# Heads' square sums as four-strip groups between the halves of a projection, and heads' row scales as one float32r product over stacked halves

## The chip, the cores and the metric

The kernel runs on one core of one Trainium2 chip. The metric is device time of one execution in microseconds (us), lower is better. A core has TensorE (PE: matrix products, which land in PSUM), VectorE (DVE), ScalarE (ACT), GpSimd (POOL) and the sync engine (SP), which here only issues transfers. Each engine works through its own list of instructions in order; engines wait for one another by semaphores. An instruction that waits holds up everything behind it on its engine.

## The reference, cut to what matters

One decoder layer for 512 prompt rows and 64 sample rows (576 together) that share weights. The part that the change touches is the QK norm of the attention branch: every head of q (16) and k (4) is scaled, row by row, by one over the root of the mean of its 64 squares.

```python
def rmsnorm(x, w):
    xf = x.astype(jnp.float32)
    y = xf * lax.rsqrt(jnp.mean(xf * xf, axis=-1, keepdims=True) + RMS_EPS)
    return (y * w.astype(jnp.float32)).astype(x.dtype)
...
z, xbc, dt_raw, q, k, v, f_raw, g_ssd, g_att = split_combined(xn @ p['w_in'])
...
q = rmsnorm(q.reshape(b, L, ATT_HEADS, ATT_HEAD_DIM), p['q_norm'])
k = rmsnorm(k.reshape(b, L, KV_HEADS, ATT_HEAD_DIM), p['k_norm'])
```

## The kernel before, in words

Activations lie transposed: 128 channels on the partitions, the 576 rows along the free axis, cut into two halves of 288. A projection multiplies a 128-column weight tile (split by `split` into float32r halves `whi` and `wlo`) with the activations (`xh`, `xl`): `mm3` (lines 207 to 215) issues three products for each of eight tiles of the contraction, 24 for each half of the rows, at lines 212, 213 and 214. These "main" products are most of PE's work all through the program. `project` (line 664) calls `mm3` for the two halves, each into its own PSUM tile `acc`, and DVE moves each half out, times the row scale `rbc` (line 669).

Ten projections make 128-channel tiles of two heads each: two of k, then eight of q (here: pair 0 to pair 9), then two tiles of v. After each of the ten, `squares` has ACT square the tile: the prompt columns into a tile of 512 columns (`Ls`, line 682), the sample columns into 64 columns of `kk` (line 683). After pairs 3, 7 and 9 it writes the products that sum the squares of each head (line 689): for each pair one full-float32 product of a 128x32 selector (`hE`, in `cst`) with the 512 columns, and one with the 64, each into its own strip of 32 PSUM partitions: pair j goes to strip j mod 4. Below, "strip product" is such a product with 512 columns.

From the sums DVE makes one over the root (`rsqrt`, line 766 on: `hs_`, transposes, `xr_`, result `yr` or `PT`). PE transposes that back to 24 partitions x 576 (lines 771 and 774), DVE copies it into `hr` (float32). `headnorm` (line 700) spreads two heads' rows of `hr` over 128 partitions by a float32 product with a 24x128 selector (line 703, 512 columns), and DVE multiplies the tile by it (line 704). It is called for the two k tiles and for q tile 0 before the attention loop, and for q tiles 1 to 7 inside it, one in every fourth step. The 64 sample columns of the two k tiles (line 787) and of all eight q tiles (line 817) are done before the loop, four times two products for q.

While this chain runs, PE is kept busy by further projections (`beside`): pieces of the gate and z projections are issued as filler. The Tile scheduler decides the order on each engine from a cost model, with `soon()` raising priority and `behind(a, b)` forbidding a ahead of b; inside the attention loop PE's order is the written one (`manual_schedule`).

Of the kernel before, what the change touches and what calls it, by code (L numbers as in the profile page):

```python
# [14 lines left out]
F32 = mybir.dt.float32  # L15
F32R = mybir.dt.float32r
I32 = mybir.dt.int32
AF = mybir.ActivationFunctionType
ALU = mybir.AluOpType
# [4 lines left out]
P = 128  # L24
OFFSET = 3000
D = 1024
NP = 512
NS = 64
NT = NP + NS
# [64 lines left out]
def build(ctx, tc, A, O):  # L94
    nc = tc.nc
    uid = [0]

    def tl(pool, shape, dt=F32, tag=None, bufs=None):
        uid[0] += 1
        kw = {} if bufs is None else {"bufs": bufs}  # L100
        return pool.tile(shape, dt, tag=tag, name=f"{tag}_{uid[0]}", **kw)
# [4 lines left out]
    mm = nc.tensor.matmul  # L106
    act = nc.scalar.activation
    V = nc.vector
    G = nc.gpsimd
# [12 lines left out]
    ident = tl(constp, [P, P], tag="ident")  # L122
    nc.scalar.dma_start(out=ident, in_=A["consts"][:, :P])

    def C(n, rows=P):
        o, w = COFF[n]
        return cst[:rows, o - P:o - P + w]
# [4 lines left out]
    def tr():  # L132
        return bank("tr", 2)

    def sm():
        return bank("mm", 2)

    def pv():
        return bank("pv", 2)
# [13 lines left out]
    def behind(later, first):  # L153

        tc.add_manual_dep(later.ins, first.ins.name, mybir.DependencyInfo(mybir.DependencyClass.NoSync, mybir.DependencyReason.DATA), reason="order")
# [51 lines left out]
    def mm3(out, w, xs, half, first=True, last=True):  # L207

        n = len(w)
        for i, ((hi, lo), (xh, xl)) in enumerate(zip(w, xs)):  # L210
            a, b = xh[:, hs(half)], xl[:, hs(half)]
            mm(out, lhsT=hi, rhs=a, start=first and i == 0, stop=False)  # L212
            mm(out, lhsT=hi, rhs=b, start=False, stop=False)  # L213
            end = mm(out, lhsT=lo, rhs=a, start=False, stop=last and i == n - 1)  # L214
        return end
# [202 lines left out]
    with pool("h1", reuse_waits="tile") as hp:  # L418
        hts = [tl(hp, [P, NT], tag=f"h{k}") for k in range(8)]
        nrm1 = Norm(0)  # L420
        with pool("xin", side="right", reuse_waits="tile") as xi:
# [4 lines left out]
            for half in range(2):  # L426
                d = slice(half * (D // 2), (half + 1) * (D // 2))
                for c in range(5):
                    n = P if c < 4 else NS
# [5 lines left out]
            t = tr()  # L435
            nc.tensor.transpose(t[:, :8], r1, ident[:8, :8])
            V.tensor_copy(P1[:, :8], t[:, :8])
            for k in range(8):
                t = tr()
# [6 lines left out]
                t = sm()  # L446
# [5 lines left out]
            for c in range(5):  # L452
                n = P if c < 4 else NS
# [6 lines left out]
        with pool("setup2", side="right", reuse_waits="tile") as su:  # L460
            q = nc.scalar
# [14 lines left out]
            t = tr()  # L476
# [7 lines left out]
            t = tr()  # L484
# [7 lines left out]
            t = tr()  # L492
# [87 lines left out]
    xs, rbc = nrm2.xs, nrm2.r  # L580
# [21 lines left out]
    with pool("dtf", side="right", reuse_waits="tile") as dp:  # L602
        w = []
        for k in range(0, 8, 4):
# [3 lines left out]
            hi, lo = split(stg, 4, 48)  # L608
            w += [(hi[:, i, :], lo[:, i, :]) for i in range(4)]
        x0 = tl(dp, [48, NT], tag="x0")  # L610
        for half in range(2):
            a = pv()
# [5 lines left out]
        e = tl(dp, [48, NT], tag="e")  # L618
# [23 lines left out]
        for c in range(5):  # L642
            n = P if c < 4 else NS
            t = tr()
# [17 lines left out]
    with pool("att", side="right", reuse_waits="tile") as ap:  # L662

        def project(w, out):
            for half in range(2):
                a = acc()
                mm3(a, w, xs, half)
                with soon():
                    V.tensor_tensor(out[:, hs(half)], a, rbc[:, hs(half)], ALU.mult)

        hp_, hq_ = pv(), sm()
        nhead = [0]

        sqs = tl(ap, [P, 10, NS], tag="kk", bufs=3)
        sqp = []

        def squares(kf):

            j = nhead[0]
            nhead[0] += 1  # L680
            sqp.append(tl(ap, [P, NP], tag="Ls", bufs=7))
            act(sqp[j], kf[:, :NP], AF.Square)
            act(sqs[:, j, :], kf[:, NP:], AF.Square)
            if j % 4 < 3 and j < 9:
                return
            for out, sq in ((hp_, lambda i: sqp[i]), (hq_[:, :NS], lambda i: sqs[:, i, :])):
                for i in range(j // 4 * 4, j + 1):
                    c, m = i % 4, i // 4
                    mm(out[c * 32:(c + 1) * 32], lhsT=C("hE")[:, 18 - 2 * m:50 - 2 * m], rhs=sq(i), start=m == 0, stop=i > 5)

        def row_of(j):
            return j % 4 * 6 + j // 4 * 2

        def heads(j, tag="bias", bufs=4):

            sel = tl(ap, [24, 2, 64], tag=tag, bufs=bufs)
            G.tensor_copy(sel, ident[:24, row_of(j):row_of(j) + 2].unsqueeze(2).to_broadcast([24, 2, 64]))
            return sel.rearrange("k e m -> k (e m)")

        def headnorm(kf, sel, wcol):  # L700
# [5 lines left out]
        def tokens(src, dst_p, dst_s, keep):  # L706
# [12 lines left out]
                res.append(o)  # L719
            return res  # L720

        kc, vc = Cols(win, CK), Cols(win, CV)
        kfs = []
        for p in range(2):
# [5 lines left out]
        for p in range(2):  # L730
            for g2 in range(0, 4, 2):
# [9 lines left out]
                for gi in range(2):  # L741
                    w = []
# [18 lines left out]
        t, t2 = tr(), sm()  # L761
# [3 lines left out]
        V.tensor_copy(xr_[:, :4], t.rearrange("p (c q r) -> p c q r", c=4, q=4)[:, :, :, :6])  # L765
        V.tensor_copy(xr_[:, 4], t2[:, :P].rearrange("p (q r) -> p q r", q=4)[:, :, :6])
        yr = rsqrt(xr_.rearrange("p c q r -> p (c q r)"), 120, ap, (("L", 4), ("PT", 2), ("Ls", 7)))
        hr = tl(ap, [24, NT], tag="hr")
        t = tr()
        for c in range(4):  # L770
            nc.tensor.transpose(t[:24, c * P:(c + 1) * P], yr[:, c * 24:(c + 1) * 24], ident)
        V.tensor_copy(hr[:, :NP], t[:24])
        t = tr()
        nc.tensor.transpose(t[:24, :P], yr[:, 96:120], ident)
        V.tensor_copy(hr[:, NP:], t[:24, P - NS:P])
        sel8 = tl(ap, [24, 8, 2, 64], tag="vv", bufs=3)
        for j, n in ((2, 2), (4, 4), (8, 2)):
            o = row_of(j)
            G.tensor_copy(sel8[:, j - 2:j - 2 + n], ident[:24, o:o + 6 * n].rearrange("k (q r) -> k q r", r=6)[:, :, :2]
                          .unsqueeze(3).to_broadcast([24, n, 2, 64]))  # L780
        khat, khs, sels = kfs, [], []
        for p in range(2):
            sels.append(heads(p))
# [772 lines left out]
```

## Time and profile before

| what | value |
|---|---|
| median of 3 runs | 1865.89 us (1864.46 to 1866.64) |
| the profiled execution | 1864.62 us, of which the trace's span is 1862.8 us |
| granted TensorE clock, mean | 0.996 of full |
| DVE, ACT, POOL busy | 56%, 41%, 34% of the span |

Times in the trace count from the span's start. A row of the timeline gives start, length, engine, line, operation, output <- inputs, shapes and how many records it merges ("x2"); in square brackets the idle time of the engine just before it and what ended that. Matrix products overlap in PE's pipeline, so what one costs is the distance between starts, not its length: six main products from 494.53 to 495.33 are 0.133 us each, though each row says 0.29. A full-float32 product leaves two records, a float32r product one.

The part of the program spoken of: pairs 0 to 9 are projected up to 541 us, v up to 548, filler from there to 605 (with `hr` ready at 573.6), then the attention loop up to about 870.

### The profile page before, as it was taken

How to read it: one execution, taken by the hardware profiler on the slowest of the kernel's cores; microseconds unless marked ns; L12 is line 12 of the kernel's file. 1: busy time of each engine (PE TensorE's matmuls, PEld its weight loads, DVE VectorE, ACT ScalarE, POOL GpSimd, SP SyncE). 2: the span in 40 equal slices, each digit the busy share in tenths (PEclk: the TensorE clock that was granted, in tenths of full speed). 3: DMA queues.
4: the chain of work that ended last, by engine and by line, in shares of the span. 5: the costliest groups of instructions: out<-in, count | busy, mean ns of one | idle time of the engine just before them, and what ended most of it. 6: DMA issues, size and time to landing. Idle time of an engine off the chain costs nothing.

```text
span 1862.8 us, 38777 instructions
## 1 busy us (share of the span) xinstructions
PE 1827.1 (98%) x15335; PEld 1724.5 (93%) x15335; DVE 1050.9 (56%) x2281; ACT 754.9 (41%) x1571; POOL 626.4 (34%) x697
## 2 busy tenths in 40 slices
PE   8999999999999999999999999989999999999998
PEld 7999999999889888888998898878999999999998
DVE  4643334443425777776737968787676454344542
ACT  4333223333323555555426555555433333123322
POOL 0433002212322445543324544746454222002210
PEclk9999999999999999999999999999999999999999
DMA  4644443344525688775356545354473344554342
GB/s 149 163 124 136 132 140 103 114 139 138 145 72 172 194 240 246 225 226 173 91 158 184 140 126 144 108 148 135 132 226 93 118 120 128 148 146 119 108 123 65
DMA packets 297723, 269.72 MB, mean 145 GB/s; under 512 B 55068, under 2 KB 262092, under 8 KB 297388
## 3 DMA queue, kind: packets, MB, share of 16 engines
q1 hardware_dynamic: 229712, 184.16, 35.0%
q10 hardware_dynamic: 57828, 46.10, 8.0%
q0 software_dynamic: 10000, 36.97, 6.2%
q8 instruction: 121, 1.98, 0.4%
q14 instruction: 62, 0.51, 0.1%
HBM read 223.72 MB, written 38.73 MB: 141 GB/s over the span
## 4 chain that ended last, share of the span: by engine, by line
PE 87%; DVE 6%; DMA 3%; ACT 2%; issue 1%; ACTq 1%; POOL 0%; SPq 0%; DVEq 0%; POOLq 0%
PE acc L212 16%; PE acc L213 16%; PE acc L214 16%; PE pv L213 8%; PE pv L212 8%; PE pv L214 8%; PE tr L962 2%; PE tr L949 1%; PE mm L885 1%; DMA ab<-cumD 1%; DVE kf L1187 1%; PE pv L916 1%; PE pv L1358 1%; PE mm L903 1%; PE pv L1000 1%
## 5 line engine op out<-in xcount | busy, mean ns | idle before, releaser
L176 ACT ACTIVATE whi<-stage 128x512 fp32r<-128x512 f32 (+2 forms) x474 | 294.3, 622 | 696.0 <-PE acc L213 606.3
L212 PE MATMUL acc<-xh,whi 128*128 128x288 f32 x1792 | 540.9, 302 | 9.0 <-DVE xr L1161 5.6
L213 PE MATMUL acc<-xl,whi 128*128 128x288 f32 x1792 | 531.2, 296 | 0.0
L214 PE MATMUL acc<-xh,wlo 128*128 128x288 f32 x1792 | 531.2, 297 | 0.0
L177 DVE TENSOR_TENSOR wlo<-stage,whi 128x512 fp32r<-128x512 f32 (+1 forms) x373 | 271.5, 728 | 251.4 <-ACT whi L176 242.6
L212 PEld LDWEIGHTS acc<-xh,whi 128*128 128x128 f32 x1792 | 337.7, 188 | 16.5 <-DVE xr L1161 7.9
L213 PEld LDWEIGHTS acc<-xl,whi 128*128 128x128 f32 x1792 | 337.9, 189 | 1.7 <-issue 1.4
L214 PEld LDWEIGHTS acc<-xh,wlo 128*128 128x128 f32 x1792 | 337.2, 188 | 2.1 <-issue 1.5
L348 POOL TENSOR_TENSOR u<-u,s 128x288 f32<-128x288 f32 x88 | 82.1, 934 | 436.6 <-DVE u L347 378.0
L177 POOL TENSOR_TENSOR wlo<-stage,whi 128x512 fp32r<-128x512 f32 (+1 forms) x101 | 138.8, 1375 | 265.7 <-ACT whi L176 248.8
L212 PE MATMUL pv<-xh,whi 128*128 128x288 f32 (+1 forms) x720 | 213.8, 297 | 0.0
L213 PE MATMUL pv<-xl,whi 128*128 128x288 f32 (+1 forms) x720 | 212.4, 295 | 0.0
L214 PE MATMUL pv<-xh,wlo 128*128 128x288 f32 (+1 forms) x720 | 212.0, 295 | 0.0
L213 PEld LDWEIGHTS pv<-xl,whi 128*128 128x128 f32 (+1 forms) x720 | 134.5, 187 | 1.3
L212 PEld LDWEIGHTS pv<-xh,whi 128*128 128x128 f32 (+1 forms) x720 | 134.6, 187 | 0.4
L214 PEld LDWEIGHTS pv<-xh,wlo 128*128 128x128 f32 (+1 forms) x720 | 134.5, 187 | 0.2
L212 PE MATMUL pv<-hh,whi 128*128 128x288 f32 x352 | 105.7, 300 | 0.0
L213 PE MATMUL acc<-hl,whi 128*128 128x288 f32 x352 | 104.1, 296 | 0.0
L212 PE MATMUL acc<-hh,whi 128*128 128x288 f32 x352 | 104.1, 296 | 0.0
L213 PE MATMUL pv<-hl,whi 128*128 128x288 f32 x352 | 104.1, 296 | 0.0
L214 PE MATMUL acc<-hh,wlo 128*128 128x288 f32 x352 | 104.1, 296 | 0.0
L214 PE MATMUL pv<-hh,wlo 128*128 128x288 f32 x352 | 103.8, 295 | 0.0
(366 smaller groups left out, 3601.7 us busy)
## 6 DMA issues: line engine op xcount, KB each, us to landing
stage<-in_w_in_dram SPq DMA_DIRECT2D x52, 512.0 KB
stage<-in_ffn_w_up_dram SPq DMA_DIRECT2D x44, 512.0 KB
stage<-in_ffn_w_gate_dram SPq DMA_DIRECT2D x43, 512.0 KB
stage<-in_ffn_w_down_dram SPq DMA_DIRECT2D x40, 512.0 KB
h<-in_state_ssm_dram SPq DMA_DIRECT2D x64, 256.0 KB
hTD<-hT ACTq DMA_DIRECT2D x32, 256.0 KB
pb<-pastD SPq DMA_DIRECT2D x32, 256.0 KB
ab<-cumD SPq DMA_DIRECT2D x32, 256.0 KB
```

What stands on the lines that cost most here:

```text
L176: act(hi, view, AF.Copy)
L177: e.tensor_tensor(lo, view, hi.bitcast(F32), ALU.subtract)
L212: mm(out, lhsT=hi, rhs=a, start=first and i == 0, stop=False)
L213: mm(out, lhsT=hi, rhs=b, start=False, stop=False)
L214: end = mm(out, lhsT=lo, rhs=a, start=False, stop=last and i == n - 1)
L348: G.tensor_tensor(u, u, sil[half], ALU.mult)
L885: mm(s[:, :n], lhsT=q, rhs=ks[2 * self.p + e][:, :n], start=hl == 0, stop=hl == 1)
L903: nc.tensor.transpose(t[:, j * P:(j + 1) * P], lt[:, j * P:(j + 1) * P], ident)
L916: mm(self.ob[o:o + 32, i * P:(i + 1) * P], lhsT=vtok[j][:, v0:v0 + 32], rhs=self.pts[e][:, j * P:(j + 1) * P], start=j == 0, stop=j == i)
L949: nc.tensor.transpose(t[:, i * P:(i + 1) * P], kk[:, i, p * P:(p + 1) * P], ident)
L962: mm(s[kv * 32:(kv + 1) * 32, :], lhsT=self.q(kv), rhs=self.kT[kv // 2], start=True, stop=True)
L1000: mm(ob[kv * 32:(kv + 1) * 32, :64], lhsT=self.pt[:, i * P + kv * 32:i * P + (kv + 1) * 32], rhs=vv[:, i, kv * 64:(kv + 1) * 64], start=jq ...
```

## The change

It has two parts. First, `squares` no longer writes the strip products at once; it puts a function `emit` on a list, and the next `project` calls it between its two halves. `emit` chains its products, each `behind` the one before it, the first behind the last product of half 0, and half 1 begins behind the last of them. Second, `hr` holds float32r values on 128 partitions: rows 0 to 23 the scales rounded to float32r, rows 32 to 55 what the rounding left, the rest zero. The selectors take both (`id2` is the sum of two shifted pieces of the identity), so one float32r product over 128 partitions replaces the float32 product over 24. The stacked halves come from two DVE copies of `yr` into `y2`, five transposes with 64 output rows, an ACT copy and a DVE subtraction.

```diff
 def mm3(...):
-            mm(out, lhsT=hi, rhs=a, start=first and i == 0, stop=False)
+            begin = mm(out, lhsT=hi, rhs=a, start=first and i == 0, stop=False)
+            if i == 0:
+                mm3.begin = begin
...
         def project(w, out):
             for half in range(2):
                 a = acc()
-                mm3(a, w, xs, half)
+                end, begin = mm3(a, w, xs, half), mm3.begin
+                if half == 0 and strips:
+                    end = strips.pop()(end)
+                elif half == 1:
+                    behind(begin, before)
+                before = end
...
         def squares(kf):
...
-            for out, sq in ((hp_, lambda i: sqp[i]), (hq_[:, :NS], lambda i: sqs[:, i, :])):
-                for i in range(j // 4 * 4, j + 1):
-                    c, m = i % 4, i // 4
-                    mm(out[c * 32:(c + 1) * 32], lhsT=C("hE")[:, 18 - 2 * m:50 - 2 * m], rhs=sq(i), start=m == 0, stop=i > 5)
+            def emit(x):
+                for out, sq in ((hp_, lambda i: sqp[i]), (hq_[:, :NS], lambda i: sqs[:, i, :])):
+                    for i in range(j // 4 * 4, j + 1):
+                        c, m = i % 4, i // 4
+                        y = mm(out[c * 32:(c + 1) * 32], lhsT=C("hE")[:, 18 - 2 * m:50 - 2 * m], rhs=sq(i), start=m == 0, stop=i > 5)
+                        behind(y, x)
+                        x = y
+                return x
+            strips.append(emit)
...
         def heads(j, tag="bias", bufs=4):
-            sel = tl(ap, [24, 2, 64], tag=tag, bufs=bufs)
-            G.tensor_copy(sel, ident[:24, row_of(j):row_of(j) + 2].unsqueeze(2).to_broadcast([24, 2, 64]))
+            sel = tl(ap, [P, 2, 64], F32R, tag=tag, bufs=bufs)
+            G.tensor_copy(sel, id2[:, row_of(j):row_of(j) + 2].unsqueeze(2).to_broadcast([P, 2, 64]))
...
+        hr = tl(ap, [P, NT], F32R, tag="hr")
+        G.memset(hr.bitcast(F32)[64:], 0.0)
+        y2 = tl(ap, [P, 5, 64], tag="Ls", bufs=7)
+        G.memset(y2, 0.0)
+        id2 = tl(ap, [P, 32], tag="id2")
+        G.tensor_tensor(id2, ident[:, :32], ident[:, 32:64], ALU.add)
+        sel8 = tl(ap, [P, 8, 2, 64], F32R, tag="vv", bufs=3)
...
-        hr = tl(ap, [24, NT], tag="hr")
-        t = tr()
-        for c in range(4):
-            nc.tensor.transpose(t[:24, c * P:(c + 1) * P], yr[:, c * 24:(c + 1) * 24], ident)
-        V.tensor_copy(hr[:, :NP], t[:24])
-        t = tr()
-        nc.tensor.transpose(t[:24, :P], yr[:, 96:120], ident)
-        V.tensor_copy(hr[:, NP:], t[:24, P - NS:P])
-        sel8 = tl(ap, [24, 8, 2, 64], tag="vv", bufs=3)
...
+        for e in range(2):
+            V.tensor_copy(y2[:, :, 32 * e:32 * e + 24], yr.rearrange("p (c r) -> p c r", c=5))
+        t, t2 = tr(), tr()
+        for c in range(5):
+            nc.tensor.transpose(t[:64, c * P:(c + 1) * P] if c < 4 else t2[:64, :P], y2[:, c, :], ident)
+        for o, v in ((hr[:, :NP], t), (hr[:, NP:], t2[:, P - NS:P])):
+            act(o[:64], v[:64], AF.Copy)
+            V.tensor_tensor(o[32:64], v[32:64], o[32:64].bitcast(F32), ALU.subtract)
```

PE's list of before, at the first group: half 1 of pair 4 (`acc_5862`) has begun when the strip products of pairs 0 to 3 come (`Ls_5604`, `Ls_5668`, `Ls_5742`, `Ls_5806`); `kk_5538` is the tile with the sample columns.

```order
L214 MATMUL acc_5862<-xh_4810,wlo_5828 128x288
L689 MATMUL pv_5536<-Ls_5604,cst_75 32x512
L689 MATMUL mm_5537<-kk_5538,cst_75 32x64
L212 MATMUL acc_5862<-xh_4910,whi_5827 128x288
L689 MATMUL pv_5536<-Ls_5668,cst_75 32x512
L213 MATMUL acc_5862<-xl_4911,whi_5827 128x288
L689 MATMUL mm_5537<-kk_5538,cst_75 32x64
L214 MATMUL acc_5862<-xh_4910,wlo_5828 128x288
L212 MATMUL acc_5862<-xh_5002,whi_5827 128x288
L213 MATMUL acc_5862<-xl_5003,whi_5827 128x288
L689 MATMUL pv_5536<-Ls_5742,cst_75 32x512
```

PE's list of the changed kernel at the same place: the last product of half 0 of pair 4 (`acc_5838`), the group, then half 1 (`acc_5872`).

```order
L216 MATMUL acc_5838<-xh_5359,wlo_5834 128x288
L700 MATMUL pv_5536<-Ls_5614,cst_75 32x512
L700 MATMUL pv_5536<-Ls_5678,cst_75 32x512
L700 MATMUL pv_5536<-Ls_5752,cst_75 32x512
L700 MATMUL pv_5536<-Ls_5816,cst_75 32x512
L700 MATMUL mm_5537<-kk_5538,cst_75 32x64 x4
L212 MATMUL acc_5872<-xh_4717,whi_5829 128x288
```

The four strip products stand together, six main products earlier than the first of them stood, and no main product is between them. Pairs 4 to 7 and pairs 8 and 9 are grouped likewise, where before each of these six stood alone among main products.

ACT's list of before at the same place: the squares of pairs 0 to 3 follow a weight split (`whi`) and a row of transfer issues (DMA).

```order
L649 DMA out_dram<-TT_911_5401 128x16
L176 ACTIVATE whi_5895<-stage_5822 128x512
L682 ACTIVATE Ls_5604<-qy_5539 128x512
L683 ACTIVATE kk_5538<-qy_5539 128x64
L682 ACTIVATE Ls_5668<-qy_5607 128x512
L683 ACTIVATE kk_5538<-qy_5607 128x64
L682 ACTIVATE Ls_5742<-qy_5689 128x512
```

ACT's list of the changed kernel there.

```order
L651 DMA out_dram<-TT_911_5401 128x16
L176 ACTIVATE whi_5905<-stage_5824 128x512
L691 ACTIVATE kk_5538<-qy_5549 128x64
L691 ACTIVATE kk_5538<-qy_5617 128x64
L690 ACTIVATE Ls_5614<-qy_5549 128x512
L690 ACTIVATE Ls_5678<-qy_5617 128x512
L690 ACTIVATE Ls_5752<-qy_5699 128x512
```

What stands ahead of the squares is as before; only two of the short squares have moved ahead of the first two long ones.

PE's list of before at the scales of the two k tiles, between main products of the filler (`acc_6713`): two products with 512 columns and two with 64.

```order
L212 MATMUL acc_6713<-xh_4910,whi_6629 128x288
L703 MATMUL tr_6443<-hr_6427,bias_6441 128x512
L703 MATMUL tr_6448<-hr_6427,bias_6446 128x512
L787 MATMUL mm_6451<-hr_6427,bias_6441 128x64
L787 MATMUL mm_6451<-hr_6427,bias_6446 128x64
L213 MATMUL acc_6713<-xl_4911,whi_6629 128x288
```

PE's list of the changed kernel there (`acc_6722` is the same half of the same filler).

```order
L215 MATMUL acc_6722<-xl_5186,whi_6642 128x288
L719 MATMUL tr_6452<-hr_5539,bias_6450 128x512
L719 MATMUL tr_6457<-hr_5539,bias_6455 128x512
L810 MATMUL mm_6460<-hr_5539,bias_6450 128x64
L810 MATMUL mm_6460<-hr_5539,bias_6455 128x64
L216 MATMUL acc_6722<-xh_5185,wlo_6643 128x288
```

The products are as many, ten main products later in the filler. `hr` and the selectors are now float32r, which the list does not show.

More of the change, by code (lines that the diff above doesn't have):

```diff
@@ L666, in project @@
                 a = acc()
-                mm3(a, w, xs, half)
+                end, begin = mm3(a, w, xs, half), mm3.begin
[4 more added lines that the diff above has]
+                before = end
                 with soon():
                     V.tensor_tensor(out[:, hs(half)], a, rbc[:, hs(half)], ALU.mult)
+        strips = []
         hp_, hq_ = pv(), sm()
@@ L720, in tokens @@
             return res
+        hr = tl(ap, [P, NT], F32R, tag="hr")
[5 more added lines that the diff above has]
+        sel8 = tl(ap, [P, 8, 2, 64], F32R, tag="vv", bufs=3)
+        for j, n in ((2, 2), (4, 4), (8, 2)):
+            o = row_of(j)
+            G.tensor_copy(sel8[:, j - 2:j - 2 + n], id2[:, o:o + 6 * n].rearrange("k (q r) -> k q r", r=6)[:, :, :2]
+                          .unsqueeze(3).to_broadcast([P, n, 2, 64]))
         kc, vc = Cols(win, CK), Cols(win, CV)
@@ L767, in build @@
         yr = rsqrt(xr_.rearrange("p c q r -> p (c q r)"), 120, ap, (("L", 4), ("PT", 2), ("Ls", 7)))
-        hr = tl(ap, [24, NT], tag="hr")
-        t = tr()
-        for c in range(4):
-            nc.tensor.transpose(t[:24, c * P:(c + 1) * P], yr[:, c * 24:(c + 1) * 24], ident)
-        V.tensor_copy(hr[:, :NP], t[:24])
-        t = tr()
-        nc.tensor.transpose(t[:24, :P], yr[:, 96:120], ident)
-        V.tensor_copy(hr[:, NP:], t[:24, P - NS:P])
-        sel8 = tl(ap, [24, 8, 2, 64], tag="vv", bufs=3)
[L777 to L780, printed above, removed]
+        for e in range(2):
[6 more added lines that the diff above has]
+            V.tensor_tensor(o[32:64], v[32:64], o[32:64].bitcast(F32), ALU.subtract)
         khat, khs, sels = kfs, [], []
```

## Prediction

> **What bounds the kernel now.** I read the page first, then PE by stretches of time.
>
> ```profile
> PE 1827.1 (98%) x15335; PEld 1724.5 (93%) x15335; DVE 1050.9 (56%) x2281; ACT 754.9 (41%) x1571; POOL 626.4 (34%) x697
> 503.00:547.00 44.00, 44.00 (x298) 38.36 (x296) 8.87 (x17) 11.24 (x23) 10.17 (x9) 1.00 0.38 107
> 640.00:720.00 80.00, 79.76 (x1031) 66.64 (x1024) 60.66 (x174) 46.58 (x111) 40.46 (x50) 1.00 0.76 226
> ```
>
> The first line has each engine's busy time. The others are windows: from and to, length, then busy time of PE, weight loads, DVE, ACT and POOL, the granted clock, the DMA share, GB/s. In the stretch of the square sums PE is not idle at all and in the first part of the attention loop by 0.24 us, and the next engine, DVE, is busy 76% there (60.66 of 80). So a product that leaves PE's list shortens the program by the distance that it put between its neighbours' starts, as long as no wait takes its place. I therefore count starts. Main products are 0.133 us apart.
>
> **The strip products.** Six of the ten stand alone, like this one (PE's timeline):
>
> ```profile
> 518.33 0.29 PE L214 MATMUL acc<-xh,wlo 128*128 128x288 f32 x1
> 518.55 1.04 PE L689 MATMUL pv<-Ls,cst 128*32 128x512 f32 x2
> 519.44 0.27 PE L689 MATMUL mm<-kk,cst 128*32 128x64 f32 x2
> 519.64 0.40 PE L212 MATMUL acc<-xh,whi 128*128 128x288 f32 x1
> 519.88 0.29 PE L213 MATMUL acc<-xl,whi 128*128 128x288 f32 x1
> ```
>
> From 518.33 to 519.64 is 1.31, 1.18 more than one main product, and the main product behind starts its successor after 0.24 instead of 0.13: 1.29 in all. Five such are 6.45; the sixth (pair 9) has a main product between its two products, which I put at 1.6: 8.05.
>
> How four in a row run is shown by the attention loop, whose sample scores have the same shapes (eight records are four products on four strips):
>
> ```profile
> 632.33 0.29 PE L214 MATMUL acc<-xh,wlo 128*128 128x288 f32 x1
> 632.55 1.06 PE L962 MATMUL tr<-kT,qz 128*32 128x512 f32 x8
> 633.43 0.29 PE L973 MATMUL tr<-khs,qz 128*32 128x64 f32 x8
> 633.54 0.62 PE L916 MATMUL pv<-PT,vt 128*32 128x128 f32 x16
> ```
>
> Four strips of 512 columns take 0.88 and the four of 64 take 0.11: no longer than one. From 632.33 to 633.54 is 1.08 over a main product, with the trailing 0.11 1.19. The groups of pairs 4 to 7 and of 8 and 9 cost 1.19 each, 2.4 in place of 8.05: **5.65 less**. They stand a half projection (24 x 0.133 = 3.2) behind the last pair's end; here is how long ACT takes from there (pair 7):
>
> ```profile
> 526.22 0.63 ACT L176 ACTIVATE whi<-stage 128x512 fp32r<-128x512 f32 x1 [0.97 <-PE acc L213]
> 527.33 0.24 ACT L683 ACTIVATE kk<-qy 128x64 f32<-128x64 f32 x1
> ```
>
> The split is released by the next to last product of the pair, and the last square ends 1.35 later, so some 1.8 of cover is left and the two groups should not wait.
>
> One rule of the Trainium skill speaks against this: "TensorE: Matmul & The Clock Gate", section "What overlaps and what doesn't", lets a weight load overlap a running product only where the row groups differ, and these strips all use the full 128 rows. By it eight loads would come on top (an estimate of some 0.1 us each by the trace's load rows) and a group would be nearer 2, the time some 1.7 higher; the first rival below holds that case. The row at 632.55 has the same full rows and shows none of it, so I stay with 1.19.
>
> **The first group waits.** In front of it PE waits already in before:
>
> ```profile
> 495.33 0.29 PE L214 MATMUL acc<-xh,wlo 128*128 128x288 f32 x1
> 496.70 1.05 PE L689 MATMUL pv<-Ls,cst 128*32 128x512 f32 x2 [1.07 <-ACT Ls L682]
> ...
> 503.01 0.40 PE L214 MATMUL acc<-xh,wlo 128*128 128x288 f32 x1
> ```
>
> Between 495.33 and 503.01 lie nine main starts: 7.68 - 1.20 = 6.5, with the trailing 0.11 6.6. In the changed order the group is reached six products earlier, at 495.33 - 5 x 0.133 = 494.66, and needs the fourth square. Why the squares come late (ACT's timeline; ACTq is its issue of transfers):
>
> ```profile
> 494.31 1.09 ACTq L649 DMA_DIRECT2D out_dram<-TT  x1
> 495.50 0.63 ACT L176 ACTIVATE whi<-stage 128x512 fp32r<-128x512 f32 x1 [3.55 <-DVE qy L669]
> ...
> 498.03 0.61 ACT L682 ACTIVATE Ls<-qy 128x512 f32<-128x512 f32 x1
> ```
>
> ACT's issue of transfers ends at 495.40 and the split starts behind it. This does not depend on PE, and ACT's list up to there is unchanged; the swap of two short squares leaves the fourth long one at 498.03. So it ends at 498.64, the fourth strip starts near 498.7, and half 1 near 498.7 + 0.89 + 0.2 = 499.8: 5.1 after 494.66, 5.2 with the trailing part. The group costs 5.2 in place of 6.6, **1.4 less**, although PE's wait grows from 1.07 to about 2 (until the first square at 496.9) and strips then dribble in.
>
> That gap may lower the clock. This trace has the granted clock around PE's gaps:
>
> ```profile
> 1040.69:1044.10 3.41, 1.51 (x19) 1.27 (x20) 3.41 (x7) 3.41 (x10) 1.96 (x3) 1.00 0.35 81
> 1044.10:1047.51 3.41, 3.41 (x25) 2.38 (x21) 3.21 (x7) 2.88 (x8) 1.57 (x4) 0.50 0.20 52
> 1146.51:1149.92 3.41, 1.97 (x15) 1.67 (x14) 2.38 (x8) 2.04 (x4) 2.06 (x4) 1.00 0.01 2
> ```
>
> A stretch with 1.51 busy of 3.41 was followed by 3.41 us at half clock; one with 1.97 busy was not. The new gap leaves some 1.4 busy of 3.41 if one such stretch holds all of it. Then the fourth strip and the main products behind it run at half speed up to 3.4 us after the gap: I estimate **1.3 more**, about as likely as not, and I count it. The Trainium skill, "TensorE: Matmul & The Clock Gate", section "What's actually happening", lowers the clock after at least one idle stretch of about 3.4 us; by that a gap of 2 us would cost nothing and the time would be 1.3 lower. The row at 1040.69 was not idle throughout and the clock fell, so the measurement decides against that reading.
>
> **The head scales.** The rows of the two k tiles, of one of the four places for q's sample columns, and of one of the seven in the loop:
>
> ```profile
> 575.86 0.29 PE L212 MATMUL acc<-xh,whi 128*128 128x288 f32 x1
> 576.09 1.98 PE L703 MATMUL tr<-hr,bias 24*128 24x512 f32 x4
> 577.91 0.55 PE L787 MATMUL mm<-hr,bias 24*128 24x64 f32 x4
> 578.39 0.40 PE L213 MATMUL acc<-xl,whi 128*128 128x288 f32 x1
> ...
> 590.47 0.65 PE L817 MATMUL mm<-hr,vv 24*128 24x64 f32 x4
> 591.05 0.40 PE L212 MATMUL acc<-xh,whi 128*128 128x288 f32 x1
> ...
> 617.24 0.29 PE L214 MATMUL acc<-xh,wlo 128*128 128x288 f32 x1
> 617.46 1.12 PE L703 MATMUL tr<-hr,PN 24*128 24x512 f32 x2
> 618.51 1.07 PE L962 MATMUL tr<-kT,qz 128*32 128x512 f32 x8
> ```
>
> And float32r products of 512 columns, which take one record each:
>
> ```profile
> 634.09 1.19 PE L885 MATMUL mm<-Ks,qs 128*128 128x512 f32 x4
> 635.12 0.30 PE L212 MATMUL acc<-xh,whi 128*128 128x288 f32 x1
> ```
>
> Four take 1.03, so 0.25 each. One with 64 columns is not in the trace; it lies between nothing and the 0.133 of a main product, and I take 0.08. Main products are float32r too, so the change of kind with its leading 0.09 and trailing 0.11 falls away.
> - k: 575.86 to 578.39 is 2.40 over a main product, 2.5 with the trailing part; new 2 x 0.25 + 2 x 0.08 = 0.7: 1.8 less.
> - q tile 0, as one of the loop's, but with main products on both sides: 1.14 + 0.11 = 1.25; new 0.25: 1.0 less.
> - q's sample columns: 590.47 to 591.05 is 0.58, with the leading 0.09 and the trailing 0.11 0.78, four times 3.1; new 8 x 0.08 = 0.6: 2.5 less.
> - the loop: 617.24 to 618.51 is 1.14, of which the next float32 product keeps its 0.09; new 0.25: 0.8 less, seven times 5.6.
>
> Together **10.9 less**. The five transposes cost the same (the moving side stays 128 columns). DVE gets two small copies more, ACT a copy, POOL's selectors are as many. The filler hides them:
>
> ```profile
> 573.39 0.20 DVE L775 COPY hr<-tr 24x64 f32<-24x64 f32 x1
> ```
>
> `hr` ends at 573.59, PE comes to the k scales 2.5 us later (576.09), and ten main products (1.3) later still in the new order. Were that cover gone, each us of the chain would cost one. POOL's gathers and weight splits keep their places to within 2 us.
>
> **Sum.** 5.65 + 1.4 - 1.3 + 10.9 = 16.7 off the profiled execution's 1864.6: 1847.9. The median of the runs lies 1.3 above that execution, so on its scale I forecast 1865.9 - 16.7 = **1849.2**.
>
> **Rivals.**
> - The strips run one after another. Against it stands 632.55; for it, that each strip here waits for a square of its own. Groups two and three then cost 0.89 for each strip and 0.3: 6.0 in place of 2.4, and the first ends 0.9 later: 4.5 more, 1853.7. Chance 0.11.
> - The loop gives its 5.6 back: a shorter step waits for another engine. For it, DVE is 76% busy there and the head scale covers ACT's copy of the keys. Against it, that copy is done at 616.5, before the product at 617.46 even starts:
>
> ```profile
> 615.47 1.06 ACT L951 ACTIVATE kT<-tr 128x512 f32<-128x512 f32 x2
> ```
>
>   It gives 1854.8. Chance 0.13.
> - The float32r product over 128 partitions is no cheaper than the float32 one over 24, so the change does not do what it says: 10.9 is lost, 1860.1. Against it stands 634.09. Chance 0.05.
> - Slower: ACT's transfer issues hold the squares, and PE now stands still until the fourth, one us for one. The gain is used up when the fourth square ends 16.7 later than 498.64, which is fifteen more issues of 1.09 like the one at 494.31; 24 later gives 1873. Nothing in the change lengthens the queue. Chance 0.03.
>
> **How the numbers follow.** The forecast has 0.62; 0.06 is left for what I have not thought of. The unknown costs: no fall of the clock gives 1847.9, free 64-column products 1848.4, dearer ones (0.133) 1849.7; a first group one us earlier or later moves it by one. The three low ends together give 1846.1, and the lowest run of before lies 1.4 under its median, so the range begins at 1844.5. It takes in the two likelier rivals, 1854.8 at most, and 2 us of a wait at the k scales beside them, and ends at 1857. A measurement of this kernel tells about 0.2% from no change (3.7 us). Faster by that: the forecast and the first three rivals, less what is unforeseen, 0.90; within it 0.06; slower 0.04.
>
> **What would show it.** Right: the first group's first strip waits about 2 us for ACT's square, and the clock falls to half once near 498 or not at all; groups two and three show eight records in under 1 us; the head scales show one record and some 0.25 between neighbours; PE stays at 98%. Wrong: strips 0.9 apart, a new wait of PE in the loop on DVE or ACT, a second wait at the k scales on DVE's subtraction.

## Result and the profile after

| | time, us | ratio to before, 95% interval |
|---|---|---|
| before, 4 runs | 1865.18 (1864.08 to 1866.64) | |
| changed kernel, 4 runs | 1847.01 (1844.81 to 1848.47) | 0.9901 [0.9884, 0.9918] |
| forecast | 1849.2 (1844.5 to 1857) | |

The profiled execution of the changed kernel took 1847.42 us (span 1845.7, mean granted clock 0.999), 17.2 less than that of before; the sum had said 16.7. PE's line of the page, and PE's waits in the attention loop (who waited, for what, us in total, times, longest):

```profile
PE 1804.6 (98%) x15315; PEld 1716.5 (93%) x15315; DVE 1048.1 (57%) x2283; ACT 755.7 (41%) x1573; POOL 628.8 (34%) x700
PE tr L985 <- ACT kT L974: 1.0, 2, 0.6
PE tr L1012 <- DVE mxs L987: 0.3, 1, 0.3
```

PE is busy 22.5 us less and still 98% of the span, so the program is bound by what it was bound by, and the loop has no new wait of any size: before had 1.5 and 0.3 us at the same two places. The second group of strips, in PE's timeline:

```profile
526.94 0.29 PE L216 MATMUL acc<-xh,wlo 128*128 128x288 f32 x1
527.16 1.06 PE L700 MATMUL pv<-Ls,cst 128*32 128x512 f32 x8
528.04 0.29 PE L700 MATMUL mm<-kk,cst 128*32 128x64 f32 x8
528.27 0.40 PE L212 MATMUL acc<-xh,whi 128*128 128x288 f32 x1
```

Eight records start within 0.88 us and nothing waits: 1.33 between the neighbours, 1.20 over a main product, 1.30 with the trailing part. The third group costs 1.29. The head scales of the two k tiles, of one of q's four sample places, and of one step of the loop:

```profile
572.13 0.30 PE L215 MATMUL acc<-xl,whi 128*128 128x288 f32 x1
572.26 0.62 PE L719 MATMUL tr<-hr,bias 128*128 128x512 f32 x2
572.73 0.30 PE L810 MATMUL mm<-hr,bias 128*128 128x64 f32 x2
572.87 0.38 PE L216 MATMUL acc<-xh,wlo 128*128 128x288 f32 x1
...
582.36 0.30 PE L216 MATMUL acc<-xh,wlo 128*128 128x288 f32 x1
582.49 0.30 PE L840 MATMUL mm<-hr,vv 128*128 128x64 f32 x2
582.63 0.38 PE L212 MATMUL acc<-xh,whi 128*128 128x288 f32 x1
582.85 0.30 PE L215 MATMUL acc<-xl,whi 128*128 128x288 f32 x1
...
607.12 0.29 PE L216 MATMUL acc<-xh,wlo 128*128 128x288 f32 x1
607.25 0.40 PE L719 MATMUL tr<-hr,PN 128*128 128x512 f32 x1
607.58 0.64 PE L985 MATMUL tr<-kT,qz 128*32 128x512 f32 x4
```

One record for each product. The k tiles cost 0.61 over a main product (0.69 with the trailing part), a sample place 0.14 and then 0.09, a step of the loop 0.46 - 0.13 = 0.33 where it was 1.14.

Only the first group is not as drawn. PE's timeline:

```profile
495.23 0.29 PE L216 MATMUL acc<-xh,wlo 128*128 128x288 f32 x1
497.34 2.32 PE L700 MATMUL pv<-Ls,cst 128*32 128x512 f32 x7 [1.81 <-ACT Ls L690]
499.05 0.48 PE L700 MATMUL mm<-kk,cst 128*32 128x64 f32 x6
499.50 0.59 PE L700 MATMUL pv<-Ls,cst 128*32 128x512 f32 x1
501.31 0.30 PE L700 MATMUL mm<-kk,cst 128*32 128x64 f32 x2 [1.22 <-ACT kk L691]
501.53 0.40 PE L212 MATMUL acc<-xh,whi 128*128 128x288 f32 x1
```

ACT at the same time (four rows; ACTq is its issue of a transfer):

```profile
495.84 0.63 ACT L176 ACTIVATE whi<-stage 128x512 fp32r<-128x512 f32 x1 [1.88 <-PE acc L216]
...
498.38 0.61 ACT L690 ACTIVATE Ls<-qy 128x512 f32<-128x512 f32 x1
500.35 0.59 ACTq L651 DMA_DIRECT2D out_dram<-TT  x1
501.00 0.26 ACT L691 ACTIVATE kk<-qy 128x64 f32<-128x64 f32 x1 [2.01 <-DMA acsD<-TT]
```

(The split's bracket names PE, but ACT's issue of a transfer ends only at 495.74, 0.10 ahead of it.) The long strips run as drawn: the first waits 1.81 for its square, the fourth square ends at 498.99 and its strip follows. But the fourth pair's short square stands on ACT behind the issue of the last transfer, which only ends at 500.94, and the short strip waits 1.22 more for it. Most of the delay is not the issue itself, which lasts 0.59. ACT stands still for 1.36 ahead of it, because the issue waits on a semaphore that the transfer of `acsD` issued at 490.73 raises; the trace has that transfer's last part landing at 500.33, and the issue starts at 500.35. In before the same transfer landed at 497.99 and the issue started at 498.01. From 495.23 to 501.53 is 6.30, 6.17 over a main product and 6.28 with the trailing part. The clock stayed at 1.00.

### The profile page after: what moved, and what is told of

The parts are those of the page before. It is cut to its first block, busy times and chain, and to the rows that moved or that the text cites. A ratio compares the mean times of both kernels' runs of the same rounds, so it can differ in the third digit from the quotient of the medians.

```text
span 1845.7 us, 38747 instructions
## 1 busy us (share of the span) xinstructions
PE 1804.6 (98%) x15315; PEld 1716.5 (93%) x15315; DVE 1048.1 (57%) x2283; ACT 755.7 (41%) x1573; POOL 628.8 (34%) x700
## 4 chain that ended last, share of the span: by engine, by line
PE 85%; DVE 5%; DMA 5%; ACT 2%; issue 1%; POOL 1%; ACTq 0%; SPq 0%; DVEq 0%; POOLq 0%
PE acc L212 16%; PE acc L215 16%; PE acc L216 16%; PE pv L216 8%; PE pv L215 8%; PE pv L212 8%; PE tr L985 2%; DMA ab<-cumD 1%; PE tr L972 1%; PE mm L908 1%; PE pv L939 1%; PE mm L926 1%; PE pv L1381 1%; PE pv L1023 1%; PE tr L387 1%
## 5 line engine op out<-in xcount | busy, mean ns | idle before, releaser
L177 DVE TENSOR_TENSOR wlo<-stage,whi 128x512 fp32r<-128x512 f32 (+1 forms) x373 | 263.4, 706 | 251.0 <-ACT whi L176 241.0
```

The costliest lines, as they stand in the source:

```text
L177: e.tensor_tensor(lo, view, hi.bitcast(F32), ALU.subtract)
```

## The experiments

All times are medians of a set's runs, beside the kernel before in the same set, whose median was 1866.68, 1868.46 and 1868.60 in the three sets.

| kernel | time, us | ratio to before, 95% interval |
|---|---|---|
| strips alone | 1861.52 | 0.9967 [0.9954, 0.9980] |
| scales alone | 1854.82 | 0.9940 [0.9924, 0.9957] |
| scales stacked, in float32 | 1859.24 | 0.9954 [0.9937, 0.9970] |
| first group a projection later | 1846.21 | 0.9893 [0.9868, 0.9918] |
| changed kernel, second set | 1847.82 | 0.9901 [0.9875, 0.9927] |
| squares a step earlier | 1845.66 | 0.9894 [0.9868, 0.9920] |
| transfers on SP's queue | 1842.71 | 0.9878 [0.9851, 0.9904] |
| strip by strip | 1846.57 | 0.9900 [0.9871, 0.9928] |
| strips twice (one run) | 1853.86 | |
| changed kernel, third set | 1849.96 | 0.9902 [0.9886, 0.9919] |
| transfers on SP's queue, third set | 1843.21 | 0.9858 [0.9844, 0.9872] |

Since these intervals are up to 0.6% wide, the sizes below are read from the traces, as distances between starts at the places themselves. A second reading is the length of whole stretches in the traces, against the one trace of before; minus is shorter. They go from start to start of PE's products: the first with `ssq` (the input's square sums), the first transpose of `yr`, the loop's first and last transpose of `kk`, the last one of `accs`.

| stretch | changed | changed, second set | strips alone | scales alone | stacked, float32 |
|---|---|---|---|---|---|
| input product to the transposes (strips) | -5.3 | -5.4 | -5.9 | +0.5 | -7.1 |
| transposes to the loop (scales of k and q) | -5.5 | -5.5 | +0.1 | -5.6 | -2.5 |
| the loop (7 scales) | -6.6 | -2.2 | +2.5 | -3.4 | +2.0 |
| from there to the last products | -0.4 | -1.6 | +3.3 | -2.0 | +3.8 |

### The two parts alone

Strips alone takes the head scales back to 24 rows of float32; scales alone takes the order of the square sums back.

```diff
-            sel = tl(ap, [P, 2, 64], F32R, tag=tag, bufs=bufs)
+            sel = tl(ap, [24, 2, 64], tag=tag, bufs=bufs)
...
-        hr = tl(ap, [P, NT], F32R, tag="hr")
+        hr = tl(ap, [24, NT], tag="hr")
```

> The strips as in the changed kernel, the head scales as before (float32 products over 24 partitions). Theory (PE is the bound, and a term is worth the distance between the starts of its neighbours): groups two and three stand as in the changed kernel, eight records in under 1 us, 1.3 from neighbour to neighbour, in place of 8.05 for the lone ones; the first group costs 6.3 with its two waits, in place of 6.6. That makes 5.75 less than the kernel before, some 1859.4 us. The head scales cost what they did (k 2.5, sample columns 0.78 each, loop products two records of 1.1). Rival (the two parts help each other, or one takes the other's place in a wait): the strips alone give under 3 us or over 8.

```diff
-                end, begin = mm3(a, w, xs, half), mm3.begin
-                if half == 0 and strips:
-                    end = strips.pop()(end)
...
+                mm3(a, w, xs, half)
```

> The strips as before (one pair at a time where the order puts them), the head scales as in the changed kernel. Theory: k 0.7, tile 0 0.25, sample columns 0.23 each, loop products one record of 0.4: 10.6 to 10.9 less than the kernel before, some 1854.5 us, and together with the kernel that has the strips alone the sum is the whole change. Rival (the loop or the k scales have a wait that the strips' earlier end covers in the changed kernel): 5 to 8 less, with a wait of PE at the k scales on DVE's subtraction or in the loop.

By medians 5.2 and 11.9 less than before, 17.1 together; the whole change gave 18.2 at first and 20.6 and 18.6 in the other sets. By places: the second and third group stand in strips alone as in the changed kernel, the k tiles of scales alone cost 0.69 and a sample place 0.23. Neither part leans on the other, and neither rival shows: no wait at the k scales in either. (The 0.5 that scales alone loses in the first row goes with a wait of 0.7 for a short square in its first group.) The first group cost 6.2 in strips alone, as expected, but in another way. There the clock did fall (windows: from and to, length, busy time of PE, weight loads, DVE, ACT and POOL, granted clock, DMA share, GB/s):

```profile
495.27:498.68 3.41, 1.33 (x10) 1.03 (x9) 0.46 (x1) 1.40 (x4) 0.69 (x1) 1.00 0.66 216
498.68:502.09 3.41, 3.41 (x14) 1.25 (x13) 0.00 (x0) 1.89 (x6) 2.51 (x3) 0.50 1.11 269
```

At half clock the long strips lasted past ACT's last issue, and the second wait had nothing left to show.

The loop's row of the table is the one that misleads. The later traces all have waits there that the first traces of before and after lack:

```profile
PE tr L972 <- DVE ys L1047: 1.5, 5, 0.3
PE tr L985 <- ACT kT L974: 1.3, 2, 0.7
PE pv L939 <- issue: 0.8, 2, 0.4
PE tr L996 <- issue: 0.6, 2, 0.4
PE tr L1012 <- DVE mxs L987: 0.3, 1, 0.3
```

This is the changed kernel in the second set: 4.5 us of waits against 1.3 in its first trace, from the same instructions. Strips alone, whose loop is that of before, has them too and is 2.5 longer than before's first trace. Among traces of the later sets it is fairer: 2.5 + 3.4 = 5.9 between strips alone and scales alone, 2.5 + 2.2 = 4.7 between strips alone and the changed kernel. The other seven later traces with the new scales lie between these two; of the old loop there is only this one later trace.

### Which half of "stacked float32r" pays

```diff
-        hr = tl(ap, [P, NT], F32R, tag="hr")
+        hr = tl(ap, [P, NT], tag="hr")
...
-        sel8 = tl(ap, [P, 8, 2, 64], F32R, tag="vv", bufs=3)
+        sel8 = tl(ap, [P, 8, 2, 64], tag="vv", bufs=3)
```

> The changed kernel with the halves and selectors in float32 in place of float32r: still stacked over 128 partitions, still the longer chain, the same number of products. Theory (the kind of number sets the product's cost): two records for each product again, 1.05 to 1.14 for 512 columns, and the change of kind between neighbours is back; 10.6 to 10.9 more than the changed kernel, some 1857.8 us. Rival (the 128 partitions or the merged copies are what pays): within 2 us of the changed kernel, 1847.

The k tiles in PE's timeline:

```profile
570.01 0.30 PE L215 MATMUL acc<-xl,whi 128*128 128x288 f32 x1
570.15 1.88 PE L719 MATMUL tr<-hr,bias 128*128 128x512 f32 x4
571.86 0.55 PE L810 MATMUL mm<-hr,bias 128*128 128x64 f32 x4
572.23 0.38 PE L216 MATMUL acc<-xh,wlo 128*128 128x288 f32 x1
```

Two records for each product are back, but not the whole price. The first product starts 0.14 behind the main product ahead of it and not 0.23. The k tiles cost 2.17 where before had 2.50, tile 0 of q 0.86 (1.24), a sample place 0.44 (0.78), a step of the loop 0.95 (1.14). Over all places stacking alone gives 2.0 outside the loop and 1.3 in it, 3.4 of the 10.7; the kind of number gives the other 7.3. The expectation had put all of it on the kind: right in the main, too high by the 3.4 as the places have it. The median does not settle this: at 12.2 above the changed kernel's first it is nearer to the expectation. Of the 11.3 between the profiled execution and that of the changed kernel's second set, 5.4 lie behind the loop, where both kernels do the same; why is not known.

### What the first group waits for

Four kernels change only what stands around it.

First, the group one projection later:

```diff
-                if half == 0 and strips:
+                if half == 0 and strips and nhead[0] != 4:
```

> The changed kernel with the first group of strips one projection later (between the halves of the projection after next; 48 main products, 6.4 us, later), all else as it is. Theory (the first group's 6.3 is waiting for ACT's squares, which stand behind ACT's issues of transfers, and not the strips): the group costs 1.3 like the other two, PE waits for no square, and the time is 5.0 lower, some 1842 us. Rival (the wait belongs to the stretch, and comes back at the next thing that PE needs from ACT or DVE, such as a weight split): the time is within 1 us of the changed kernel, 1847, with a wait of 2 to 5 us elsewhere between 495 and 515.

PE's timeline, around the group and the start of half 1:

```profile
500.94 0.29 PE L216 MATMUL acc<-xh,wlo 128*128 128x288 f32 x1
501.15 1.07 PE L700 MATMUL pv<-Ls,cst 128*32 128x512 f32 x8
...
503.28 0.40 PE L212 MATMUL acc<-xh,whi 128*128 128x288 f32 x1 [0.95 <-DVE qy L676]
```

No strip waits for a square, and the group runs like the others. But a wait of 0.95 appears right behind it, for the copy that frees the accumulator: the place costs 2.3, 4 less and not 5. The rival had a part of it. The median, 0.8 under the changed kernel's first, is too loose to show that.

Second, the squares a step earlier in ACT's list:

```diff
-            act(sqp[j], kf[:, :NP], AF.Square)
-            act(sqs[:, j, :], kf[:, NP:], AF.Square)
+            with soon():
+                act(sqp[j], kf[:, :NP], AF.Square)
+                act(sqs[:, j, :], kf[:, NP:], AF.Square)
```

> The changed kernel with the squares issued a step earlier in ACT's list, so that the fourth short square of the first group stands ahead of the last two issues of transfers and not behind them. Theory (the second wait, 1.2 us on the short square, is ACT's issue of transfers): that wait is gone, the first group costs 4.4 to 5.2 in place of 6.3, the time is 1.2 lower than the changed kernel of this set. Rival (the short square is late for another reason, or the time goes into the first wait): the first group still costs over 6.

ACT's fourth short square and its last issue:

```profile
496.65 0.24 ACT L692 ACTIVATE kk<-qy 128x64 f32<-128x64 f32 x1
498.05 0.58 ACTq L651 DMA_DIRECT2D out_dram<-TT  x1
```

The short square is ahead of the last issue, and the second wait is gone: 4.85 in place of 6.2. The first wait is as it was, 1.79.

Third, the ten transfers that ACT issued, on SP's queue:

```diff
-            nc.scalar.dma_start(out=acsD[c * P:c * P + n], in_=TT[c][:n, 64:96])
+            nc.sync.dma_start(out=acsD[c * P:c * P + n], in_=TT[c][:n, 64:96])
...
-            nc.scalar.dma_start(out=dst, in_=TT[c][:n, 32:48])
+            nc.sync.dma_start(out=dst, in_=TT[c][:n, 32:48])
```

> The changed kernel with the ten transfers that ACT issues ahead of and between the first squares put on SP's queue. Theory (ACT's issues of transfers make the squares late, and the square sums themselves cost 1.3): ACT's weight split and squares run 2 to 4 us earlier, the first group costs 1.3 to 2.5 with at most one wait under 1.2, and the time is 4 to 5 lower, some 1842 us. Rival (the squares are late because of their input, or the transfers cost the same wherever they are issued, for SP's loads of the k weights then come late): the first group still waits over 2 us, or PE waits for a weight split behind it, and the time is within 1 us of the changed kernel.

PE's timeline in that kernel:

```profile
492.55 0.29 PE L216 MATMUL acc<-xh,wlo 128*128 128x288 f32 x1
492.77 1.07 PE L700 MATMUL pv<-Ls,cst 128*32 128x512 f32 x8
...
493.88 0.40 PE L212 MATMUL acc<-xh,whi 128*128 128x288 f32 x1
```

And ACT's fourth long square:

```profile
492.06 0.62 ACT L690 ACTIVATE Ls<-qy 128x512 f32<-128x512 f32 x1
```

Against PE's position ACT is some 3.6 earlier (its fourth long square starts 0.49 ahead of the last main product, and it started 3.15 behind it). Both waits are gone and the group costs 1.3, 5.0 less. Nothing behind it waits instead. Run again beside the changed kernel, with more rounds:

> The changed kernel with the ten transfers on SP's queue, once more and in more rounds, as the version to beat. Theory: the first group costs 1.3 again and the time is 4 to 5.5 below the changed kernel beside it. Rival (its lower median was chance of the session): within 2 us of it.

> The changed kernel once more, as the neighbour of the run with the transfers on SP's queue: 1847.5 within 2 us, the first group 4.5 to 6.5.

1.3 again; the medians are 5.1 and 6.8 under the changed kernel of the same set, of which the place gives 5.0; the rest of the 6.8 is not explained. Whether the issues' own length or their waiting for earlier transfers makes the first square late, this kernel does not tell apart: it takes both off ACT. This version beats both kernels: 0.9858 of before [0.9844, 0.9872].

Fourth, the changed kernel itself, for what one execution tells of the next:

> The changed kernel once more, beside the others of this set. Theory (what differs between two executions of it is chance: which gaps of PE lower the clock, and when ACT's and SP's transfers are issued): 1847 us within 3, groups two and three of the strips and the head scales as in its first trace (1.3, 0.69, 0.23) within 0.05, and the first group anywhere from 4.5 to 6.5. Rival (the terms hold in one execution only): a term of the scales or of groups two and three off by more than 0.2.

The scales and the two free groups repeat within 0.02 at every place. The first group repeats in sum but not in kind:

| execution | wait for the first square | second wait | clock | cost of the group |
|---|---|---|---|---|
| changed, first | 1.81 | 1.22 | 1.00 | 6.3 |
| changed, second set | 1.81 | 1.14 | 1.00 | 6.2 |
| changed, third set | 2.34 | none | half | 6.2 |
| strips alone | 2.08 | none | half | 6.2 |
| stacked, float32 | 1.20 | none | 1.00 | 4.5 |

In the other three kernels that have the group at this place (squares a step earlier, strip by strip, strips twice) the clock held there too.

### What a group of strips is limited by

```diff
-                for out, sq in ((hp_, lambda i: sqp[i]), (hq_[:, :NS], lambda i: sqs[:, i, :])):
-                    for i in range(j // 4 * 4, j + 1):
+                for i in range(j // 4 * 4, j + 1):
+                    for out, sq in ((hp_, lambda i: sqp[i]), (hq_[:, :NS], lambda i: sqs[:, i, :])):
```

> The changed kernel with the products of a group in another order: the 512 columns and the 64 of one strip, then those of the next strip. Same products, same place, still with no other product between them. Theory (four products overlap when the next in line has another strip; a product on the same strip waits for the one before it): each strip takes about 0.9 + 0.1 by itself, groups of four cost 3.7 to 4.2 in place of 1.3 and the group of two 2.0 to 2.2; with the first group, which waits for its squares anyway, up 0.5 to 1, the time is 4 to 5 higher than the changed kernel of this set. Rival (standing together is what pays, since the change of kind between products falls away): groups of four still 1.3 to 1.6, the time within 1 us.

The second group in PE's timeline:

```profile
523.03 0.29 PE L216 MATMUL acc<-xh,wlo 128*128 128x288 f32 x1
523.25 1.08 PE L700 MATMUL pv<-Ls,cst 128*32 128x512 f32 x8
524.13 0.32 PE L700 MATMUL mm<-kk,cst 128*32 128x64 f32 x8
524.37 0.40 PE L212 MATMUL acc<-xh,whi 128*128 128x288 f32 x1
```

The expectation was wrong: 1.34 between the neighbours, as in the changed kernel. In the list a short product of strip 0 stands between the long products of strips 0 and 1, yet all long ones start first and the short ones follow together. So the order inside a group does not matter when its squares are there (the first group, which waits for them, cost 6.1 here); that nothing else stands in it does. The next kernel then doubled each strip's work:

```diff
+                        for e in range(2):
-                        y = mm(out[c * 32:(c + 1) * 32], lhsT=C("hE")[:, 18 - 2 * m:50 - 2 * m], rhs=sq(i), start=m == 0, stop=i > 5)
+                            y = mm(out[c * 32:(c + 1) * 32], lhsT=C("hE")[:, 18 - 2 * m:50 - 2 * m], rhs=sq(i), start=m == 0 and e == 0, stop=i > 5 and e == 1)
```

> The changed kernel with every strip product of the square sums issued twice in a row on its own strip, the second adding to the first, so the square sums come out doubled and the heads' scales with them. It measures what a group of strips is limited by. Theory after the strip-by-strip run (each strip works through its own products, and one that has to wait does not hold up the next strip's): each strip takes 2 x 0.9 for its 512 columns, all four beside each other, 16 records in 1.8; groups two and three cost 1.0 more each, 2.3. Rival, the one that run spoke against (products run in list order, and one that waits for its strip holds back those behind it): the four strips go in five steps of 0.9, the two strips in three, groups of 4.9 and 3.1. Second rival (a strip does not limit at all, records only follow each other): 1.3 to 1.5.

Its second group:

```profile
526.07 0.29 PE L216 MATMUL acc<-xh,wlo 128*128 128x288 f32 x1
526.29 1.94 PE L701 MATMUL pv<-Ls,cst 128*32 128x512 f32 x16
528.03 0.44 PE L701 MATMUL mm<-kk,cst 128*32 128x64 f32 x16
528.40 0.40 PE L212 MATMUL acc<-xh,whi 128*128 128x288 f32 x1
```

Sixteen records in 1.74, the groups cost 2.3 and 2.3: each strip works through its own two products, and the four strips side by side. A lone strip therefore costs as much as four (0.89 of start distance in before, 0.88 for four). That the main products on both sides are 128 columns wide and cannot stand beside a strip is the likely reason; no run tests it by itself.

## Why the prediction was right, point by point

- **PE bounds, so distances count.** Right: 17.2 came off the profiled time where the sum of distances said 16.7, and PE stayed at 98%. The places as measured add up to 16.5: 5.5 by the two free groups, 0.3 by the first, 10.7 by the head scales.
- **Second and third group 2.4 in place of 8.05.** Right: 1.30 + 1.29 = 2.6, without waits. The 0.1 each that is missing lies between the short products and the main product behind them: 0.23 (528.04 to 528.27) where the loop's row had 0.11 (633.43 to 633.54), and there the next product was a float32 strip again. The trailing part had been counted. The rival of strips one after another would have been 6.0; strip by strip and strips twice show why it is not.
- **First group 5.2 in place of 6.6, and 1.3 more for the clock.** The sum held (6.3 against 6.5) and the mechanism did not. The step that failed is "the swap of two short squares leaves the fourth long one at 498.03. So ... half 1 near 498.7 + 0.89 + 0.2": the long square was followed to its end and the short one was not. In the changed order it stands behind ACT's last issue of a transfer, and the short strips are the last thing before half 1, so they set its start. That issue is in before's timeline too, but it started 2.3 us earlier there, since the transfer that it waits for landed earlier. The kernel with the squares a step earlier takes that wait away (4.85) and the one with the transfers on SP's queue both. The clock was a fair coin priced at its full value; it fell in two of the five executions in the table above, and there it hid the second wait. That the sum held in the profiled execution was luck: the fall that was counted (1.3) did not come, and a wait that was not counted (1.22) did.
- **Head scales 10.9 less.** Right in sum: 5.0 outside the loop and 7 x 0.81 = 5.7 in it, 10.7. A 64-column product was mis-sized: it starts its neighbour after 0.07, as estimated, but the main product behind it still has a trailing 0.09, so the four sample places cost 0.9 and not 0.6. That trailing part was said to fall away with the change of kind; it stays behind a short product (behind tile 0's long one, at 576.61, there is none). The leading one fell away, but the kernel stacked in float32 starts 0.14 after the main product too, so it does not go with the kind. It goes with the shape: products of 24*128 start 0.23 after a main product and the strips' 128*32 start 0.22 after one, those of 128*128 0.13 to 0.14, in either kind.
- **The filler hides the longer chain.** Right: no wait at the k scales, in any run.
- **The loop gives 5.6 back.** Not so: 6.6 less in the first pair of traces, 4.7 to 5.9 less among later ones. But waits on the engines that the rival named differ between executions, with or without the change: for the keys' copy `kT` from none to 2.1 us, and for DVE's `ys` 1.4 to 1.5 in all eleven later traces and none in the first two. What makes them come was not found.
- **The float32r product is no cheaper.** Not so, though a third of the gain is not its doing.

The median lies 2.2 under the forecast: 0.5 is the sum, 0.7 is the median of before, which was 1865.9 when the forecast was made and 1865.2 with one run more, and the other 1.0 is less than the spread of either kernel's runs.

## What to carry to other kernels

When a group of products waits for several results of another engine, follow the last result that the group needs to its end, short ones too, through everything queued ahead of it there; transfers issued by that engine count, and so does the landing of an earlier transfer that such an issue waits for. Products on different strips of the array should stand together with no full-width product between them: four then cost what one does. And a product with fewer rows than its neighbours can be cheaper when zeros fill it up to their shape, apart from what its kind of number costs: here that was 3.4 of 10.7.

## What the runs showed of the hardware

**The clock falls on a grid.** In every trace that has several falls, they start a whole number of steps of 3.413 us apart and last one step or two (one at the program's end is cut short): in strips alone at 498.68, 1044.81 and 1239.37, 160 and 217 steps from the first. Over the grid's steps the fall follows a step in which PE was busy for less than about half of it:

```profile
493.17:496.59 3.42, 1.61 (x13) 1.38 (x12) 1.62 (x4) 1.60 (x5) 0.90 (x1) 1.00 0.52 164
496.59:500.00 3.41, 2.64 (x14) 0.56 (x13) 0.00 (x0) 1.54 (x4) 3.26 (x8) 1.00 1.01 280
1131.47:1134.88 3.41, 1.80 (x14) 1.49 (x13) 2.31 (x7) 1.93 (x4) 2.17 (x5) 1.00 0.01 2
1134.88:1138.29 3.41, 3.41 (x16) 3.41 (x15) 3.41 (x10) 1.33 (x2) 0.14 (x1) 0.50 0.04 8
```

This is the changed kernel in the second set: 1.61 busy was not followed by a fall and 1.80 was, so busy time is not quite the measure, and the edge lies near half a step. In all thirteen traces, from 470 to 1300 us, every step that began at full clock with 1.51 or less busy was followed by a fall, and none with more than 1.80; of the twelve between, three were. The Trainium skill, "TensorE: Matmul & The Clock Gate", section "What's actually happening", asks for an idle window of about 3.4 us; the length agrees, the idleness doesn't. A gap of 2 us therefore costs nothing or, by an estimate from the length of a step, some 1.7 us of work (half of 3.41) by where it lies on the grid. The falls alone do not explain the last row of the second table: before and strips alone both have 10.2 us at half clock behind the loop, and differ there by 3.3.

**Strips are served apart.** By the records of strip by strip, PE started a long product of strip 1 ahead of a short one of strip 0 that stands before it in the list: the long ones start from 523.2 to 523.7, the short ones from 524.1. So the engines' working through their lists in order, as said at the top, does not hold for PE's starts inside a group.
